# A transformer block's down projection: each of two large buffers holds four residual rows and eight half blocks

## The chip, the cores and the metric

The kernel runs on one core of a Trainium2 chip. A core has five engines that run side by side, each with its own instruction stream: TensorE (PE, matrix products into PSUM banks), VectorE (DVE), ScalarE (ACT), GpSimd (POOL) and SyncE (SP). They wait for each other through semaphores. Sixteen DMA engines move data between HBM and the on-chip memory (SBUF, 128 partitions); here SyncE and GpSimd issue nearly all transfers. The metric is the device time of one launch in microseconds (us), the median of several runs.

## The reference

One layer of a decoder trunk over 1024 tokens of width 1024. A gated mixing sublayer comes first; behind it stands a gated MLP with a short causal convolution, and a residual with layer norm. The change touches the last matrix product and the last two lines:

```python
def conv_ffn(h, w_up, dw_w, dw_b, w_down):
    u = causal_dwconv(h @ w_up, dw_w, dw_b)
    gate, val = jnp.split(u, 2, axis=-1)
    return (jax.nn.silu(gate) * val) @ w_down
...
ffn = conv_ffn(h, w_ffn_up[l], ffn_dw_w[l], ffn_dw_b[l], w_ffn_down[l])
h = layer_norm(DN_ALPHA * h + ffn, ln2_g[l], ln2_b[l])
```

The inner width is 2816 (22 blocks of 128), all data are float32, and `DN_ALPHA` is the fourth root of 2.

## The kernel before

**Products.** A float32 operand is held as two parts, high (a cast, by ScalarE) and low (the rest, by a subtraction on VectorE). `mm3` multiplies high by high, high by low and low by high (L170, L171, L172).

**Up phase.** `up_rest` runs 22 times (j = 0 to 21). Its results `fo` go to scratch in HBM, in a form in which the down phase needs them: `b11_scr`, `b2_scr`, `t32_scr`, `t1_scr`, issued by GpSimd (L995, L997, L1002, L1003).

**Down phase.** `down` computes `@ w_down` by Winograd's form of Strassen's scheme: seven products of half-size operands, p = 0 to 6, in place of eight. Each product has 11 steps k, and a step issues 12 matmuls, three for each of four PSUM banks (128 tokens by 512 columns each). Products 0, 2, 4 and 6 accumulate in the banks X (`acc` 452 to 455), products 1, 3 and 5 in Y (`sm` 456 to 459). After product p the banks are added to the residual rows on VectorE (`own`, L1110; `more`, L1113).

A step's operands come through `load(p, k)`: SyncE fetches a raw tile `dr` (scratch half at L1055, weight half at L1058), GpSimd fetches a second weight block `do` (L1064) for products 0, 1, 4 and 5; VectorE adds them (L1027) into a place that is kept (`c3[k]` in product 0, `c4[k]` in product 1) or in place; ScalarE casts the high part (L1092) and VectorE subtracts for the low part (L1093) of the tile `w_dn`. `dr` has five tiles in turn, so the load of step n + 5 waits until the readers of step n's tile are done. `do` has four, two of them in a pool with the up phase's tiles `s`.

**Big buffers.** A pool `big` holds two buffers of 4 MB each. In the down phase the first holds the eight residual rows (`rows`, read back from `h1_scr` at L1022, eight transfers of 0.5 MB); the second holds the eleven kept blocks `c3`; the `c4` blocks have tiles of their own. Each buffer becomes free when the up phase's tile in it (`h1b1`, `h1b2`) has been read for the last time. The third tile, `last`, takes the next free buffer: it holds the split weights of the last four steps of product 6 (k = 7 to 10).

**The end.** Product 6 runs steps 0 to 2 over all four banks; then, bank by bank, the other eight steps, so that the banks finish one after the other. Product 5's result completes rows 0 to 3, product 6's rows 4 to 7. `ln_out` normalises a row: statistics (L211, L225), square root on ScalarE (L226), reciprocal (L227), two halves each of L231 and L234, and a store of each half to the output by SyncE (L1170).

**Order.** The tile framework schedules the instructions of each engine when the kernel is built, from data dependencies and the priorities in the code; on the chip every engine then keeps its order. DMAs issued by GpSimd go through one queue and those of SyncE through another.

Of the kernel before, what the change touches and what calls it, by code (L numbers as in the profile page):

```python
# [16 lines left out]
P = 128  # L17
# [38 lines left out]
def kernel(  # L56
# [101 lines left out]
    def col_weights(hh, ct):  # L158
        scr = low_scr.get(ct)
        return weights(  # L160
            wcol[ct], f"c{hh}_{ct}", None if hh else scr, scr if hh else None
        )

    def big_tile(name):
# [747 lines left out]
    def up_weights(upp, j):  # L912
# [19 lines left out]
            w3 = split_pair(upp, s3, f"s3_{j}", HALF, 2)  # L932
        return w24, w10, w3

    def up_rest(upp, bl, j, before):

        w24, w10, w3 = up_weights(upp, j)
        ug, uv = (  # L940
            upp.tile([P, T + 32], F32, tag="u", bufs=3, name=f"f{n}{j}") for n in ("ug", "uv")
        )
        s = upp.tile([P, HALF], F32, tag="s", bufs=2, name=f"s{j}")
        SY.dma_start(s, first_scr[j][0])
        SY.dma_start(ug[:, 2 : 2 + HALF], first_scr[j][1])
        G.memset(ug[:, :2], 0.0)
        G.memset(uv[:, :2], 0.0)
        ps, pz = bank(0), bank(0)
        early, late = slice(2, 2 + HALF), slice(2 + HALF, 2 + T)
# [12 lines left out]
        V.tensor_tensor(out=uv[:, early], in0=pz, in1=s, op=ALU.subtract)  # L962
        product(ps, lambda i: w24[:, i, HALF:], bl["b22"], False)
        A.copy(ug[:, late], ps)
        os = []
        j = j // 2 + j % 2 * NK
        for jj, u in ((j, ug), (NF + j, uv)):
            o = upp.tile([P, T], F32, tag="o", bufs=3, name=f"fo{jj}")
            wc = PC_FW + 3 * jj
            A.activation(  # L970
                out=o, in_=u[:, 2 : 2 + T], func=AF.Identity, scale=pc[:, wc + 2 : wc + 3]
            )
            for k in range(2):
                V.scalar_tensor_tensor(
                    out=o,
                    in0=u[:, k : k + T],
                    scalar=pc[:, wc + k : wc + k + 1],
                    in1=o,
                    op0=ALU.mult,
                    op1=ALU.add,  # L980
                )
            os.append(o)
        og, ov = os
        A.activation(out=og, in_=og, func=AF.Silu, bias=pc[:, PC_FB + j : PC_FB + j + 1])
        V.scalar_tensor_tensor(
            out=ov,
            in0=ov,
            scalar=pc[:, PC_FB + NF + j : PC_FB + NF + j + 1],
            in1=og,
            op0=ALU.add,  # L990
            op1=ALU.mult,
        )
        early, late = slice(0, HALF), slice(HALF, T)
        if j < NK:
            G.dma_start(b11_scr[j], ov[:, early])  # L995
            return ov
        G.dma_start(b2_scr[j - NK], ov)  # L997
        a, b, t = before, ov, og
        V.tensor_tensor(out=t[:, early], in0=a[:, late], in1=b[:, late], op=ALU.subtract)
        V.tensor_tensor(out=a[:, late], in0=a[:, early], in1=a[:, late], op=ALU.subtract)  # L1000
        V.tensor_tensor(out=t[:, late], in0=t[:, early], in1=a[:, early], op=ALU.subtract)
        G.dma_start(t32_scr[j - NK], t)  # L1002
        G.dma_start(t1_scr[j - NK], a[:, late])  # L1003

    def down(upp, dp):
# [6 lines left out]
        def flat_big(name):  # L1012
            return big_tile(name).bitcast(F32).rearrange("p i k t -> p (i k t)")

        rows, kept = flat_big("rows"), flat_big("c3")
        c3 = [kept[:, k * HALF : (k + 1) * HALF] for k in range(NK)]
        c4 = [dp.tile([P, HALF], F32, name=f"c4_{k}") for k in range(NK - 1)]
        c4.append(upp.tile([P, HALF], F32, tag="s3", name="c4_last"))
        rs = [rows[:, t * D : (t + 1) * D] for t in range(8)]
        sts = [dp.tile([P, 2, 6], F32, name=f"st_f{t}") for t in range(8)]  # L1020
        for t in range(8):
            G.dma_start(rs[t], h1_scr[t * P : (t + 1) * P, :])  # L1022
        g, b = (row(dp, w, D, n, eng=G) for w, n in ((RW_2G, "ln2_g"), (RW_2B, "ln2_b")))
        E, L = slice(0, HALF), slice(HALF, D)

        def add(dst, x, y):
            V.tensor_tensor(out=dst, in0=x, in1=y, op=ALU.add)  # L1027

        n_steps, n_raw, n_other = 0, 0, 0

        def raw(name):
            nonlocal n_raw
# [1 line left out]
            pl, tag, bufs = ((wst, "st", 3), (upp, "raw", 2))[n_raw % 5 in (1, 3)]  # L1034
            return pl.tile([P, D], F32, tag=tag, bufs=bufs, name=f"{name}_{n_raw}")

        last = []

        def load(p, k):

            nonlocal n_steps, n_other
            a11, a21, a12, a22 = (wdown[h * NK + k, :, cs] for h in range(2) for cs in (E, L))
            x = (
                b11_scr[k],
                b2_scr[k][:, E],
                t32_scr[k][:, L],
                t32_scr[k][:, E],
                t1_scr[k],
                b2_scr[k][:, E],
                b2_scr[k][:, L],  # L1050
            )[p]
            with tc.high_priority(offset=4000):
                st = raw("dr")
                w_st = st[:, E]
                SY.dma_start(st[:, L], x)  # L1055
                w_of = (a11, a12, a22, None, a21, a22, None)[p]
                if w_of is not None:
                    SY.dma_start(w_st, w_of)  # L1058
                o_of = (a21, a22, None, None, a22, t32_scr[k][:, L], None)[p]
                if o_of is not None:  # L1060
                    n_other += 1
                    pl, tag = ((dp, "other"), (upp, "s"))[n_other % 2]
                    other = pl.tile([P, HALF], F32, tag=tag, bufs=2, name=f"do{p}_{k}")
                    G.dma_start(other, o_of)  # L1064
                if p < 2:
                    add((c3, c4)[p][k], w_st, other)
                elif p == 2:
                    add(w_st, w_st, c3[k])
                elif p == 3:
                    w_st = c3[k]  # L1070
                    add(c4[k], c4[k], c3[k])
                elif p == 4:
                    add(w_st, w_st, other)
                elif p == 5:
                    add(st[:, L], st[:, L], other)
                else:
                    w_st = c4[k]
                if p == 6 and k >= NK - 4:
                    if not last:
                        last.append(big_tile("last").rearrange("p i k t -> p (i k t)"))  # L1080
                    w = last[0][:, (k - NK + 4) * 2 * D : (k - NK + 5) * 2 * D]
                    w = w.rearrange("p (i n) -> p i n", i=2)
                else:
                    own = n_steps % 2 and n_steps > 2
                    w = (dp if own else wsp).tile(
                        [P, 2, D], F32R, tag="w", bufs=3, name=f"w_dn{p}_{k}"
                    )
                cuts = ((slice(0, D), st),) if w_st is not c3[k] and w_st is not c4[k] else (
                    (E, w_st), (L, st[:, L])
                )  # L1090
                for cs, src in cuts:
                    A.copy(w[:, 0, cs], src)  # L1092
                    V.tensor_tensor(  # L1093
                        out=w[:, 1, cs], in0=src, in1=w[:, 0, cs].bitcast(F32), op=ALU.subtract
                    )
            n_steps += 1
            return w
# [53 lines left out]
        for p, (banks, first, then) in enumerate(products):  # L1151
            end = NK - LAST if p == 6 else NK
            for k in range(end):
                w = load(p, k)
                for t in range(4):
                    block(banks[t], w, t, first, k)
            ws = {k: load(p, k) for k in range(end, NK)}
            for t in range(4):
                for k in ws:
                    block(banks[t], ws[k], t, first, k)  # L1160
                then(t)
# [143 lines left out]
```

## Time and profile before

| | |
|---|---|
| median of 3 runs | 1967.86 us (1967.69 to 1970.54) |
| the profiled execution | 1962.23 us, of it the span that the trace covers 1960.5 us |
| busy: TensorE, its weight loads, VectorE, ScalarE, GpSimd | 98%, 80%, 82%, 55%, 11% |
| up phase ends, down phase begins | the first matmul of product 0 at 1726.81 us, the last of the up phase at about 1741 |
| last matmul begins, VectorE ends | 1949.74 us, 1957.35 us |

Times in the trace count from the start of the span. The parts of the profile that are used below: busy shares of the engines; a table of stretches of the span with the busy time of each engine, the granted TensorE clock and the load of the DMA engines; a timeline of one engine (start, duration, engine, line, operation, tiles, and in square brackets how long the engine had stood idle and which event ended that); the chain of waits, followed back from the last instruction; and the DMA transfers with their time from issue to landing. An instruction on VectorE or ScalarE shows some 0.1 us more than it keeps the engine, since it overlaps the next: a row's duration may exceed the distance of two starts. The duration 0.39 us of a matmul is its way through the engine; one starts every 0.23 us.

### The profile page before, as it was taken

How to read it: one execution, taken by the hardware profiler on the slowest of the kernel's cores; microseconds unless marked ns; L12 is line 12 of the kernel's file. 1: busy time of each engine (PE TensorE's matmuls, PEld its weight loads, DVE VectorE, ACT ScalarE, POOL GpSimd, SP SyncE). 2: the span in 40 equal slices, each digit the busy share in tenths (PEclk: the TensorE clock that was granted, in tenths of full speed). 3: DMA queues.
4: the chain of work that ended last, by engine and by line, in shares of the span. 5: the costliest groups of instructions: out<-in, count | busy, mean ns of one | idle time of the engine just before them, and what ended most of it. 6: DMA issues, size and time to landing. Idle time of an engine off the chain costs nothing.

```text
span 1960.5 us, 25846 instructions
## 1 busy us (share of the span) xinstructions
PE 1928.3 (98%) x9453; PEld 1572.2 (80%) x9453; DVE 1599.4 (82%) x2224; ACT 1083.5 (55%) x1617; POOL 216.8 (11%) x258
## 2 busy tenths in 40 slices
PE   9999999999999999999999999999999999989997
PEld 7888777777788788888778888888888888868886
DVE  7599999999887548898999646587788888879778
ACT  4666667654263266868775435365555555544432
POOL 0001000111310000110201130001000000121010
PEclk9999999999999999999999999999999999999999
DMA  7645455556446665555554744566445455588673
GB/s 265 223 167 209 162 193 183 172 167 220 142 168 205 211 218 183 191 185 196 190 173 155 233 139 129 176 248 225 167 171 185 165 198 173 184 299 296 196 227 130
DMA packets 127648, 378.36 MB, mean 193 GB/s; under 512 B 15104, under 2 KB 15648, under 8 KB 127520
## 3 DMA queue, kind: packets, MB, share of 16 engines
q1 hardware_dynamic: 107424, 318.48, 48.2%
q0 software_dynamic: 13760, 46.69, 6.9%
q10 hardware_dynamic: 6336, 11.54, 1.6%
q8 instruction: 74, 1.21, 0.2%
q14 instruction: 54, 0.44, 0.1%
HBM read 289.99 MB, written 86.65 MB: 192 GB/s over the span
## 4 chain that ended last, share of the span: by engine, by line
PE 57%; DVE 10%; DMA 5%; ACT 2%; issue 2%; SPq 0%; DVEq 0%; ACTq 0%
PE acc L172 13%; PE acc L171 13%; PE acc L170 13%; PE sm L171 5%; PE sm L172 5%; PE sm L170 5%; DVE c L453 3%; DMA dr<-wdown 1%; DMA dr<-b_scr 1%; DVE w_dn L1093 1%; DMA b_scr<-fo 1%; DVE x L408 1%; PE sm L536 1%; DVE rows L231 1%; DVE rows L234 1%
## 5 line engine op out<-in xcount | busy, mean ns | idle before, releaser
L170 PE MATMUL acc<-hT,w_c 128*128 128x512 f32 x1000 | 391.9, 392 | 0.6 <-ACT x L406 0.6
L172 PE MATMUL acc<-hT,w_c 128*128 128x512 f32 x1000 | 390.2, 391 | 0.6 <-DVE w_c L151 0.5
L171 PE MATMUL acc<-hT,w_c 128*128 128x512 f32 x1000 | 390.6, 391 | 0.0
L453 DVE SCALAR_TENSOR_TENSOR c<-v,pc,c 128x512 f32<-128x512 f32 x480 | 372.2, 801 | 7.1 <-ACT c L442 4.6
L170 PEld LDWEIGHTS acc<-hT,w_c 128*128 128x128 f32 x1000 | 187.8, 188 | 41.6 <-issue 1.9
L172 PEld LDWEIGHTS acc<-hT,w_c 128*128 128x128 f32 x1000 | 187.7, 188 | 41.4 <-DVE w_c L151 1.7
L171 PEld LDWEIGHTS acc<-hT,w_c 128*128 128x128 f32 x1000 | 187.8, 188 | 39.5 <-issue 1.1
L147 ACT CAST w_c<-st_c 128x1024 fp32r<-128x1024 f32 x128 | 133.8, 1045 | 108.9 <-PE acc L172 82.3
L515 POOL TENSOR_TENSOR ce<-ce,xbc 128x1024 f32<-128x1024 f32 x28 | 80.1, 2861 | 678.6 <-ACT ce L514 678.6
L1092 ACT CAST w_dn<-dr 128x1024 fp32r<-128x1024 f32 (+1 forms) x73 | 68.8, 945 | 86.4 <-DMA dr<-wdown 32.8
L504 ACT ACTIVATE m<-ab,acs 128x128 f32<-128x128 f32 x256 | 78.4, 390 | 48.9 <-PE sm L536 47.7
L170 PE MATMUL sm<-h1s,w_s 128*128 128x512 f32 x264 | 102.7, 389 | 0.0
L171 PE MATMUL sm<-h1s,w_s 128*128 128x512 f32 x264 | 102.7, 389 | 0.0
L172 PE MATMUL sm<-h1s,w_s 128*128 128x512 f32 x264 | 102.2, 389 | 0.0
L151 DVE TENSOR_TENSOR w_c<-st_c,w_c 128x1024 fp32r<-128x1024 f32 x64 | 79.0, 1237 | 22.3 <-ACT w_c L147 22.1
L408 DVE SCALAR_TENSOR_TENSOR x<-u,pc,x 128x512 f32<-128x512 f32 x96 | 79.7, 842 | 4.0 <-ACT x L406 3.8
L1093 DVE TENSOR_TENSOR w_dn<-dr,w_dn 128x1024 fp32r<-128x1024 f32 (+1 forms) x73 | 78.6, 1086 | 4.0 <-ACT w_dn L1092 4.0
L172 PE MATMUL acc<-h1b,w_ue 128*128 128x512 f32 x176 | 68.8, 394 | 0.2 <-DVE w_ue L151 0.2
L170 PE MATMUL acc<-h1b,w_ue 128*128 128x512 f32 x176 | 68.6, 390 | 0.0
L171 PE MATMUL acc<-h1b,w_ue 128*128 128x512 f32 x176 | 68.5, 389 | 0.0
L170 PE MATMUL sm<-h1b,w_s 128*128 128x512 f32 x176 | 68.5, 389 | 0.0
L171 PE MATMUL sm<-h1b,w_s 128*128 128x512 f32 x176 | 68.5, 389 | 0.0
(325 smaller groups left out, 4533.9 us busy)
## 6 DMA issues: line engine op xcount, KB each, us to landing
st_c<-wcol SPq DMA_DIRECT2D x128, 512.0 KB, 4.4
low_scr<-w_c SPq DMA_DIRECT2D x64, 512.0 KB, 2.9
w_c<-low_scr SPq DMA_DIRECT2D x64, 512.0 KB, 4.4
ab<-acs_scr SPq DMA_DIRECT2D x32, 512.0 KB, 4.1
dr<-wdown SPq DMA_DIRECT2D x55, 256.0 KB, 5.3
st_wo<-wo SPq DMA_DIRECT2D x24, 512.0 KB, 4.1
st_ue<-wup SPq DMA_DIRECT2D x22, 512.0 KB, 3.9
first_scr<-first ACTq DMA_DIRECT2D x44, 256.0 KB, 3.0
```

Of the source, the lines that this page charges most:

```text
L147: A.copy(w[:, 0, :], st)
L151: V.tensor_tensor(out=w[:, 1, :], in0=st, in1=w[:, 0, :].bitcast(F32), op=ALU.subtract)
L170: TE.matmul(ps, wa(0), xa(0), start=start, stop=False, skip_group_check=more)
L171: TE.matmul(ps, wa(0), xa(1), start=False, stop=False, skip_group_check=more)
L172: TE.matmul(ps, wa(1), xa(0), start=False, stop=stop, skip_group_check=more)
L231: V.scalar_tensor_tensor(out=t, in0=t, scalar=mv[:, i, 0:1], in1=g, op0=ALU.subtract, op1=ALU.mult)
L408: V.scalar_tensor_tensor(out=o, in0=u[:, k : k + HALF], scalar=pc[:, wc + k : wc + k + 1], in1=o, op0=ALU.mult, op1=ALU.add,)
L453: V.scalar_tensor_tensor(out=accs[i], in0=v[:, k : k + HALF], scalar=pc[:, wc + k : wc + k + 1], in1=accs[i], op0=ALU.mult, op1=ALU.add,)
L504: A.activation(out=m[:, h, :], in_=ab[:, h, :], func=AF.Relu, scale=-1.0, bias=acs[:, c, 8 * g + h : 8 * g + h + 1],)
L515: G.tensor_tensor(out=ce, in0=ce, in1=CT[:, cs].unsqueeze(1).to_broadcast([P, 8, P]), op=ALU.mult)
L1092: A.copy(w[:, 0, cs], src)
L1093: V.tensor_tensor(out=w[:, 1, cs], in0=src, in1=w[:, 0, cs].bitcast(F32), op=ALU.subtract)
```

## The change

- Two tiles `rows_c3` and `rows_c4` take the two big buffers. Each holds four residual rows (0 to 3, and 4 to 7) in its first half and eight half blocks in its second: `c3[0]` to `c3[7]` in the first buffer; `c3[8]` to `c3[10]` and `c4[0]`, `c4[1]` in the second. The rest of `c4` keeps tiles of its own.
- Only rows 0 to 3 are loaded at the start. Rows 4 to 7 are loaded in product 2, at its steps 1, 3, 5 and 7, and the two rows of the layer norm (`ln2_g`, `ln2_b`) in product 4. A new function `issue_after` puts each of them behind the newest `do` load in GpSimd's order; it sets the order only, without a semaphore.
- The `do` loads get four buffers of their own in the down phase's pool, and none in the up phase's.
- The last `b11` store (`b11_scr10`) is issued behind the fourth `do` load.
- The weight tile of the fourth step is allocated ahead of all others (`w_dn_own`).

The core of the diff; `issue_after` and the list `stores` are shown at its start, the calls of `load_row` and `load_norm` at its end.

```diff
+    def issue_after(later, earlier):
+
+        tc.add_manual_dep(
+            later.ins,
+            earlier.ins.name,
+            mybir.DependencyInfo(mybir.DependencyClass.NoSync, mybir.DependencyReason.DATA),
+            reason="issue order",
+        )
...
-            G.dma_start(b11_scr[j], ov[:, early])
+            stores.append(G.dma_start(b11_scr[j], ov[:, early]))
...
-        rows, kept = flat_big("rows"), flat_big("c3")
-        c3 = [kept[:, k * HALF : (k + 1) * HALF] for k in range(NK)]
-        c4 = [dp.tile([P, HALF], F32, name=f"c4_{k}") for k in range(NK - 1)]
+        slots = [flat_big(n) for n in ("rows_c3", "rows_c4")]
+        pieces = [[s[:, k * HALF : (k + 1) * HALF] for k in range(8, 16)] for s in slots]
+        c3 = pieces[0] + pieces[1][:3]
+        c4 = pieces[1][3:5]
+        c4 += [dp.tile([P, HALF], F32, name=f"c4_{k}") for k in range(2, NK - 1)]
         c4.append(upp.tile([P, HALF], F32, tag="s3", name="c4_last"))
-        rs = [rows[:, t * D : (t + 1) * D] for t in range(8)]
+        rs = [slots[t // 4][:, t % 4 * D : (t % 4 + 1) * D] for t in range(8)]
         sts = [dp.tile([P, 2, 6], F32, name=f"st_f{t}") for t in range(8)]
-        for t in range(8):
-            G.dma_start(rs[t], h1_scr[t * P : (t + 1) * P, :])
-        g, b = (row(dp, w, D, n, eng=G) for w, n in ((RW_2G, "ln2_g"), (RW_2B, "ln2_b")))
+        g, b = (dp.tile([P, D], F32, name=n) for n in ("ln2_g", "ln2_b"))
+        first_own = dp.tile([P, 2, D], F32R, tag="w", bufs=3, name="w_dn_own")
+
+        def load_row(t):
+            i = G.dma_start(rs[t], h1_scr[t * P : (t + 1) * P, :])
+            if t >= 4:
+                issue_after(i, others[-1])
+
+        for t in range(4):
+            load_row(t)
+
+        def load_norm():
+            for r, start in ((g, RW_2G), (b, RW_2B)):
+                i = G.dma_start(r, prow[start : start + D].partition_broadcast(P))
+                issue_after(i, others[-1])
+
...
-                    n_other += 1
-                    pl, tag = ((dp, "other"), (upp, "s"))[n_other % 2]
-                    other = pl.tile([P, HALF], F32, tag=tag, bufs=2, name=f"do{p}_{k}")
-                    G.dma_start(other, o_of)
+                    other = dp.tile([P, HALF], F32, tag="other", bufs=4, name=f"do{p}_{k}")
+                    others.append(G.dma_start(other, o_of))
+                    if len(others) == 4:
+                        issue_after(stores[-1], others[-1])
...
-                    )
+                    ) if n_steps != 3 else first_own
...
                 w = load(p, k)
+                if p == 2 and k % 2 and k < 8:
+                    load_row(4 + k // 2)
+                elif p == 4 and k == 1:
+                    load_norm()
```

**What it moves.** GpSimd's stream at the end of the up phase, before the change, from the load of the rows on (`fuv`, `fug` and `fo` are tiles of the up phase, `do0_k` is the second block of step k of product 0):

```order
L1022 DMA rows_14232<-h1_scr_115 128x1024 x8
L947 MEMSET fuv20_14026 128x2
L946 MEMSET fug21_14129 128x2
L997 DMA b2_scr9_169<-fo42_13959 128x1024
L1003 DMA t1_scr9_158<-fo31_13819 128x512
L1002 DMA t32_scr9_180<-fo20_13955 128x1024
L1064 DMA do0_0_14268<-wdown 128x512
L947 MEMSET fuv21_14130 128x2
L995 DMA b11_scr10_148<-fo32_14104 128x512
L1064 DMA do0_1_14289<-wdown 128x512
L1064 DMA do0_3_14331<-wdown 128x512
L207 DMA ln2_g_14261<-prow 128x1024
```

And after it:

```order
L1038 DMA rows_c3_14232<-h1_scr_115 128x1024 x4
L958 MEMSET fuv20_14026 128x2
L957 MEMSET fug21_14129 128x2
L1008 DMA b2_scr9_169<-fo42_13959 128x1024
L1014 DMA t1_scr9_158<-fo31_13819 128x512
L1013 DMA t32_scr9_180<-fo20_13955 128x1024
L958 MEMSET fuv21_14130 128x2
L1088 DMA do0_0_14261<-wdown 128x512
L1088 DMA do0_1_14282<-wdown 128x512
L1088 DMA do0_2_14303<-wdown 128x512
L1088 DMA do0_3_14324<-wdown 128x512
L1006 DMA b11_scr10_148<-fo32_14104 128x512
```

The loads of the rows are four and not eight; `do0_0` has gone behind the memset of `fuv21`, `do0_1` to `do0_3` ahead of the store of `b11_scr10`, and the two layer-norm rows are gone from here. Rows 4 to 7 stand behind `do1_10` now, and the layer-norm rows behind `do4_1`.

ScalarE's stream where product 0 begins, before (`w_dn0_0` is the weight tile of the first step, `fo10` and `fo32` are results of the up phase):

```order
L964 COPY fug20_14025<-sm448_14032 128x512
L1092 CAST w_dn0_0_14271<-dr_1_14265 128x1024
L970 ACTIVATE fo10_14100<-fug20_14025,pc_99 128x1024
L970 ACTIVATE fo32_14104<-fuv20_14026,pc_99 128x1024
L1092 CAST w_dn0_1_14292<-dr_2_14286 128x1024
L984 ACTIVATE fo10_14100<-fo10_14100,pc_99 128x1024
```

And after:

```order
L975 COPY fug20_14025<-sm448_14032 128x512
L981 ACTIVATE fo10_14100<-fug20_14025,pc_99 128x1024
L1118 CAST w_dn0_0_14264<-dr_1_14258 128x1024
L981 ACTIVATE fo32_14104<-fuv20_14026,pc_99 128x1024
L995 ACTIVATE fo10_14100<-fo10_14100,pc_99 128x1024
L970 COPY fuv21_14130<-sm450_14136 128x512
L1118 CAST w_dn0_1_14285<-dr_2_14279 128x1024
```

The activation of `fo10` has gone ahead of the cast for the first step, and the cast for the second behind the copy of `fuv21`.

ScalarE's stream behind product 3's last step, before (`w_dn3_10`; `c4_7` to `c4_last` are kept blocks of steps 7 to 10):

```order
L1092 CAST w_dn3_10_15155<-dr_44_15152 128x512
L1092 CAST last_15785<-c4_8_14242 128x512
L1092 CAST last_15785<-c4_last_14244 128x512
L1092 CAST last_15785<-c4_7_14241 128x512
L1092 CAST last_15785<-c4_9_14243 128x512
L1092 CAST w_dn4_0_15182<-dr_45_15176 128x1024
```

And at the end of product 6, before (`rs_f0` to `rs_f3` are the square roots for rows 0 to 3):

```order
L1092 CAST last_15785<-dr_75_15790 128x512
L1092 CAST last_15785<-dr_77_15802 128x512
L1092 CAST w_dn6_5_15771<-c4_5_14239 128x512
L1092 CAST w_dn6_5_15771<-dr_72_15769 128x512
L1092 CAST last_15785<-dr_76_15796 128x512
L1092 CAST w_dn6_6_15778<-c4_6_14240 128x512
L1092 CAST w_dn6_6_15778<-dr_73_15776 128x512
L226 ACT_TABLE_LOAD
L226 ACTIVATE rs_f0_15649<-mv_f0_15648,eps_95 128x1
L226 ACTIVATE rs_f1_15662<-mv_f1_15661,eps_95 128x1
L226 ACTIVATE rs_f2_15675<-mv_f2_15674,eps_95 128x1
L226 ACTIVATE rs_f3_15688<-mv_f3_15687,eps_95 128x1
```

The same engine at the same place, after:

```order
L235 ACTIVATE rs_f0_15647<-mv_f0_15646,eps_95 128x1
L235 ACTIVATE rs_f1_15660<-mv_f1_15659,eps_95 128x1
L235 ACTIVATE rs_f2_15673<-mv_f2_15672,eps_95 128x1
L235 ACTIVATE rs_f3_15686<-mv_f3_15685,eps_95 128x1
L1118 CAST last_15783<-c4_7_14239 128x512
L1118 CAST last_15783<-c4_9_14241 128x512
L1118 CAST last_15783<-c4_8_14240 128x512
L1118 CAST last_15783<-c4_last_14242 128x512
L1118 CAST last_15783<-dr_76_15794 128x512
L1118 CAST last_15783<-dr_75_15788 128x512
L1118 CAST last_15783<-dr_74_15781 128x512
L1118 CAST last_15783<-dr_77_15800 128x512
```

All eight casts into `last` now stand behind the square root for row 3. VectorE's eight subtractions into `last` stand, likewise, behind the last instruction that normalises row 3, and TensorE takes the 84 matmuls of product 6 that read other weight tiles before the 48 that read `last`.

More of the change, by code (lines that the diff above doesn't have):

```diff
@@ L933, in up_weights @@
         return w24, w10, w3
+    stores = []
     def up_rest(upp, bl, j, before):
@@ L1027, in add @@
             V.tensor_tensor(out=dst, in0=x, in1=y, op=ALU.add)
-        n_steps, n_raw, n_other = 0, 0, 0
+        n_steps, n_raw = 0, 0
         def raw(name):
@@ L1035, in raw @@
             return pl.tile([P, D], F32, tag=tag, bufs=bufs, name=f"{name}_{n_raw}")
-        last = []
+        last, others = [], []
         def load(p, k):
-            nonlocal n_steps, n_other
+            nonlocal n_steps
             a11, a21, a12, a22 = (wdown[h * NK + k, :, cs] for h in range(2) for cs in (E, L))
```

## The prediction

> **What bounds the kernel now.** First the page's busy shares, then the table of stretches for the two places where TensorE is not full.
>
> ```profile
> PE 1928.3 (98%) x9453; PEld 1572.2 (80%) x9453; DVE 1599.4 (82%) x2224; ACT 1083.5 (55%) x1617; POOL 216.8 (11%) x258
> ```
>
> ```profile
> 1720.00:1740.00 20.00, 17.28 (x75) 13.68 (x74) 13.75 (x13) 10.98 (x12) 3.36 (x7) 1.00 0.60 230
> 1740.00:1760.00 20.00, 17.32 (x73) 12.99 (x72) 18.37 (x22) 7.58 (x8) 5.47 (x10) 1.00 0.96 329
> 1760.00:1780.00 20.00, 19.49 (x85) 15.57 (x84) 17.00 (x23) 8.41 (x8) 5.20 (x10) 1.00 1.00 357
> 1780.00:1800.00 20.00, 20.00 (x90) 16.56 (x89) 20.00 (x27) 8.43 (x8) 3.55 (x7) 1.00 0.93 323
> ...
> 1920.00:1940.00 20.00, 20.00 (x90) 16.53 (x90) 20.00 (x40) 6.30 (x13) 0.00 (x0) 1.00 0.22 79
> ```
>
> Columns: stretch, length, busy time of PE, its weight loads, DVE, ACT and POOL (instructions in brackets), granted clock, DMA share, GB/s. TensorE is the bound, so time can be won only where it idles: at the start of the down phase (1720 to 1780) and behind the last matmul. From 1920 to 1940 VectorE is full as well. The timeline of PE gives the first matmul of product 0, two of the gaps, and the first of product 2; the pace of a step is read from ScalarE's casts, which TensorE there releases one step at a time.
>
> ```profile
> 1726.81 1.07 PE L170 MATMUL acc<-w_dn 128*128 128x512 f32 x4
> ...
> 1730.82 1.20 PE L170 MATMUL acc<-w_dn 128*128 128x512 f32 x4 [1.14 <-ACT w_dn L1092]
> ...
> 1750.31 1.20 PE L170 MATMUL acc<-w_dn 128*128 128x512 f32 x4 [1.00 <-ACT w_dn L1092]
> ...
> 1800.25 1.07 PE L170 MATMUL acc<-w_dn 128*128 128x512 f32 x4
> ```
>
> ```profile
> 1865.78 1.05 ACT L1092 CAST w_dn<-dr 128x1024 fp32r<-128x1024 f32 x1 [1.67 <-PE acc L172]
> 1868.50 1.05 ACT L1092 CAST w_dn<-dr 128x1024 fp32r<-128x1024 f32 x1 [1.67 <-PE acc L172]
> ```
>
> A step of 12 matmuls takes 2.72 us, one matmul 0.2267. From 1726.81 to 1800.25 TensorE runs products 0 and 1 (22 steps) and the 24 matmuls left of the up phase: 288 x 0.2267 = 65.28 of 73.44 us. **8.16 us are lost there**, and no more than these can be won. The chain of waits says by what:
>
> ```profile
> 1714.68 12.66 DMA b_scr<-fo
> 1727.50 0.47 ACT fo L970
> ...
> 1741.19 0.70 DVE c L1027
> 1741.96 0.32 SPq L1055
> 1742.33 6.82 DMA dr<-wdown
> 1749.21 1.05 ACT w_dn L1092
> ```
>
> ```profile
> 1741.19 1.29 DVE L1027 TENSOR_TENSOR c<-dr,do 128x512 f32<-128x512 f32 x2 [0.41 <-PE sm L172]
> ```
>
> Two waits. A store of the up phase (12.66 us) holds the tile that ScalarE's next activation writes. Then the first sum kept in `c3` waits for a big buffer, whose last reader is a matmul of the up phase. That sum frees the raw tile of `dr_6`, which SyncE therefore loads at 1741.96 only.
>
> **The change at the start.** GpSimd now issues four rows ahead of that store, not eight. Its timeline, the landing time of the rows, and three more stretches:
>
> ```profile
> 1708.23 4.26 POOL L1022 DMA_DIRECT2D rows<-h_scr  x8 [10.28 <-PE acc L172]
> ...
> 1725.54 0.56 POOL L1064 DMA_DIRECT2D do<-wdown  x1 [6.53 <-ACT w_dn L1092]
> ...
> 1737.38 1.09 POOL L1064 DMA_DIRECT2D do<-wdown  x2
> ```
>
> ```profile
> rows<-h_scr POOLq DMA_DIRECT2D x8, 512.0 KB, 10.6
> ```
>
> ```profile
> 1723.00:1728.00 5.00, 5.00 (x24) 4.14 (x23) 2.80 (x3) 1.66 (x3) 0.56 (x1) 1.00 1.03 416
> 1728.00:1733.00 5.00, 2.88 (x12) 1.74 (x10) 4.26 (x4) 3.29 (x4) 0.10 (x1) 1.00 0.42 160
> 1733.00:1738.00 5.00, 4.39 (x19) 3.67 (x20) 4.70 (x6) 3.08 (x4) 1.16 (x3) 1.00 0.01 6
> ```
>
> At 416 GB/s the four rows that go (2 MB) are 5.0 us of a full DMA, so the store lands near 1722.3 in place of 1727.3, and the activation that waited is no longer late. The DMA then lies idle until the loads of product 0 start (share 0.42, then 0.01): the loads had no free tiles and stood behind a store in GpSimd's queue. Now four `do` loads go ahead of the last `b11` store, at about 1728.6 to 1730.8 (GpSimd's memset that waits for the up phase's `fo` at 1732.6 before, less 4 to 5 us, stands ahead of them). They land 5 to 6 us later; the first `c3` sums run near 1736, since `c3[0]` lies in the buffer that has been free since 1708; `dr_6` goes out near 1736.7, 5.3 us earlier. TensorE, unbroken, wants its weights at 1745.9; loaded in 6.82 us and cast and subtracted in 2.2 they stand at 1745.7. Later steps have 1 to 5 us by the same count, and product 2 could begin at 1792.1. At its third step I find a new wait: VectorE must empty product 1's banks first (8.3 us of it behind 1791.0, weights at 1799.3, wanted 1798.4): 0.9 us. **Start: -7.2 us**; the bounds are -8.16 (all of it) and -3 (only the 5 us of the store's wait and what hangs on it, less ScalarE's new order, below).
>
> *Costs that I put at nothing.* Rows 4 to 7 and the two LN rows (3 MB) now ride behind the last `do` of product 1, around 1780 to 1792, beside loads that by the table fill 0.93 of the DMA before; their first reader is product 3, tens of us later, so they can cost only by delaying product 2's weights: 0 to 1 us. Issue slots on GpSimd move and do not grow. The four `other` buffers hold no work back.
>
> **The change at the end.** `last`, the big tile for the weights of the last four steps of product 6, took `c3`'s buffer, free after product 3; half of its casts ran near 1847. Now it takes the buffer of rows 0 to 3, so all 8 casts stand behind the LN of row 3 *and* the landing of the 8 stores of these rows. Rows of VectorE, TensorE, ScalarE and the stores:
>
> ```profile
> 1919.70 0.68 DVE L1113 TENSOR_TENSOR rows<-rows,sm 128x512 f32<-128x512 f32 x1
> ...
> 1938.37 0.67 DVE L1110 SCALAR_TENSOR_TENSOR rows<-rows,acc 128x512 f32<-128x512 f32 x1
> 1938.95 2.73 DVE L234 SCALAR_TENSOR_TENSOR rows<-rows,rs_f,ln_b 128x512 f32<-128x512 f32 x4
> 1941.60 0.69 DVE L211 BATCH_NORM_STATS2 st_f<-rows 128x6 f32<-128x512 f32 x1
> ...
> 1950.32 0.64 DVE L1110 SCALAR_TENSOR_TENSOR rows<-rows,acc 128x512 f32<-128x512 f32 x1
> ...
> 1955.94 1.41 DVE L234 SCALAR_TENSOR_TENSOR rows<-rows,rs_f,ln_b 128x512 f32<-128x512 f32 x2
> ```
>
> ```profile
> 1920.05 0.39 PE L170 MATMUL acc<-w_dn 128*128 128x512 f32 x1
> ```
>
> ```profile
> 1847.05 1.14 ACT L1092 CAST last<-c 128x512 fp32r<-128x512 f32 x2
> 1848.09 1.05 ACT L1092 CAST w_dn<-dr 128x1024 fp32r<-128x1024 f32 x1
> ```
>
> ```profile
> out_dram<-rows SPq DMA_DIRECT2D x16, 256.0 KB, 2.1
> ```
>
> All in before's clock, the start's gain apart. VectorE worked without a pause from 1919.70 to 1941.60, 21.9 us, until row 3 was normalised; 2.4 of them were three `last` subtractions and the first sum of `acc`, which now come later: 19.5. It begins when product 5's first bank is done, 9 matmuls ahead of 1920.05, near 1918.2, so row 3 is ready at 1937.7; its store lands 2.1 to 2.9 later, about **1940.2**. TensorE has 84 matmuls of product 6 that need no `last`: 1920.05 + 19.04 = 1939.1. Its next wants the seventh cast: 7 x 0.52 (two casts take 1.04 from 1847.05 to 1848.09) puts it at 1943.9. **TensorE stands still for 4.8 us.** Its 23rd matmul (5.2 us) completes the first bank at 1949.1. From there VectorE has all of rows 4 to 7 ahead of it: from 1950.32 to the end at 1957.35 it took 7.03, 2.7 of them row 6's, so 4.3 for row 7 with its wait for the square root, 4.0 without; 3 x 4.0 + 4.3 = 16.3. End at 1965.4, not 1957.35: **+8.1 us**; bounds +6 (store 2.0, no other loss) and +10.
>
> *The clock at the restart.* It is a term of its own. The trace has no idle TensorE in mid-kernel that long, but it has both ends:
>
> ```profile
> 1950.00:1955.00 5.00, 0.13 (x1) 0.00 (x0) 4.96 (x11) 0.59 (x2) 0.00 (x0) 0.94 0.39 145
> 1955.00:1960.50 5.50, 0.00 (x0) 0.00 (x0) 2.31 (x5) 0.00 (x0) 0.00 (x0) 0.50 0.42 155
> ```
>
> ```profile
> 3.00:4.00 1.00, 1.00 (x7) 1.00 0.97 389
> ...
> 7.00:8.00 1.00, 1.00 (x12) 1.00 0.99 381
> ```
>
> The last matmul ends at 1950.13 and the clock falls to half: 0.94 over 1950 to 1955 puts the fall near 1954.4, 4.3 us behind it. At the kernel's start (columns: PE, clock, DMA, GB/s) the same transposes run 7 in a us at first and 12 later; the slow part lasts some 4 us. An idle of 4.8 us outlasts 4.3, so I take the restart as cold: 4 us at 7/12 of the pace lose 1.7. Bounds 0 and 2. [...]
>
> **Sum**: -7.2 + 8.1 + 1.7 = **+2.6 us**. Against the profiled execution (1962.23; span 1960.5) that is 1964.8; the runs' median of 1967.86 lies 5.63 above it, for which the trace shows no cause, so I add to the median: **1970.5 us**.
>
> **Rivals.**
> [...]
> 2. *Start not won* (slower). ScalarE's new order puts the up phase's activation ahead of the cast for the very first step. It pays if the store still lands beyond about 1724.8, from where each us is a us of TensorE, up to 2.9; and the loads stay DMA-bound (0.96 to 1.00 in the table). Then the start gives 3 of 7.2: +6.8, 1974.7. Against it: 2 MB fewer on that queue, and 10 us of idle DMA to fill.
> 3. *Faster.* If the 5.63 us that the median lies over the profiled execution are lost in the same starved stretch, the change takes them as well: 2.6 - 5.6 = -3.0, or with a warm restart -4.7: 1964.9 to 1963.2. Nothing in the trace speaks for or against it.
> 4. *The order isn't kept at the end*: some casts into `last` do not wait for the stores (-2.5 us of the stall, and a warm clock): -1.6, 1966.3. Against it: they share one tile.
>
> **Chances.** Forecast 0.42, warm restart 0.20, start not won 0.20, faster 0.10, order not kept 0.08. About 0.2% (3.9 us) is what a measurement of this kernel tells from no change. Slower by more: all but a little of rival 2 and a third of the forecast's spread, 0.33; faster by more: most of rival 3 and a little else, 0.12; the rest, 0.55. The range runs from 1964.8 (rival 3's near end) to 1975.5 (rival 2 with a late store).
>
> **What would show it.** Start: no PE gap between the first matmul of product 0 and product 1; the DMA share of 1733 to 1738 far from 0.01; `dr_6` issued near 1737. End: ScalarE's eight `last` casts in a row near 1933 to 1937 (7.2 us ahead of before's clock), a PE gap of 4 to 5 us before the first matmul on `last`, the first of them 0.4 us apart where they are 0.23 warm, and VectorE ending some 27 us behind the landing of row 3's last store. It is wrong if the gap is under 3 us, or if product 0 still shows gaps of 1 us and more.

## The result, and the profile after

| | before | changed |
|---|---|---|
| median of 22 runs each | 1964.5 us (1960.59 to 1970.54) | 1969.5 us (1965.7 to 1975.55) |
| ratio, 95% interval | 1 | 1.0026 (1.0017 to 1.0034) |
| profiled execution's span | 1960.5 us | 1964.0 us |
| product 0's first matmul to product 6's first (185.1 without a gap) | 193.24 us | 188.11 us |
| product 6's first matmul to VectorE's end | 37.30 us | 47.51 us |

The change makes the kernel 5.1 us slower (0.26% of 1964.5). The last two rows say where: **the start of the down phase gains 5.1 us, its end loses 10.2**; the sum is the measured 5.1. The spans differ by 3.5 only because this execution of the changed kernel reached product 0 1.5 us sooner, at a place that the change doesn't touch.

The start, in the table of stretches of the changed kernel (columns as above):

```profile
1720.00:1740.00 20.00, 19.47 (x87) 15.79 (x86) 18.00 (x19) 13.18 (x14) 4.46 (x9) 1.00 0.51 166
1740.00:1760.00 20.00, 20.00 (x90) 16.57 (x89) 19.91 (x23) 8.94 (x9) 5.60 (x11) 1.00 0.99 345
1760.00:1780.00 20.00, 20.00 (x90) 16.57 (x89) 18.67 (x25) 8.55 (x9) 6.05 (x12) 1.00 0.97 351
1780.00:1800.00 20.00, 18.27 (x81) 14.47 (x79) 18.57 (x26) 5.64 (x6) 3.57 (x7) 1.00 1.03 388
```

PE is full from 1740 to 1780, where it lost time before. New is the gap in the last row, beside a DMA share of 1.03. PE's timeline has all that is left of the start's loss, and product 6's first matmul:

```profile
1725.31 1.07 PE L179 MATMUL acc<-w_dn 128*128 128x512 f32 x4
...
1728.72 0.50 PE L179 MATMUL sm<-h1s,w_s 128*128 128x512 f32 x1 [0.53 <-ACT fuv L970]
...
1797.64 1.21 PE L179 MATMUL acc<-w_dn 128*128 128x512 f32 x4 [0.63 <-ACT w_dn L1118]
1799.95 0.50 PE L180 MATMUL acc<-w_dn 128*128 128x512 f32 x1 [1.09 <-DVE w_dn L1119]
...
1913.42 0.39 PE L179 MATMUL acc<-w_dn 128*128 128x512 f32 x1
```

Counted from start to start the three gaps cost 0.8, 0.8 and 1.5 us (a gap in brackets leaves out the slower start behind it: from the first matmul to the second 0.34 us, at 1728.72 and at 1799.95, where others start 0.23 apart), some 3 us where 8.1 were lost before. At the end the chain of waits goes row by row through the path that the change added:

```profile
1928.54 2.73 DVE rows_c L243 x4
1931.29 2.08 DMA out_dram<-rows_c
1933.62 3.75 ACT last L1118 x7
1937.40 0.50 PE acc L179
```

VectorE normalises rows 2 and 3, the last of their stores lands, ScalarE makes seven casts, and only then TensorE runs on. PE's and VectorE's timelines of the same stretch:

```profile
1937.40 0.50 PE L179 MATMUL acc<-last 128*128 128x512 f32 x1 [4.78 <-ACT last L1118]
1937.74 0.59 PE L180 MATMUL acc<-last 128*128 128x512 f32 x1
1938.13 0.63 PE L179 MATMUL acc<-last 128*128 128x512 f32 x1
1938.56 0.63 PE L180 MATMUL acc<-last 128*128 128x512 f32 x1
...
1941.12 0.44 PE L179 MATMUL acc<-last 128*128 128x512 f32 x1
1941.39 0.39 PE L180 MATMUL acc<-last 128*128 128x512 f32 x1
1941.63 0.40 PE L181 MATMUL acc<-last 128*128 128x512 f32 x1
```

```profile
1944.56 0.69 DVE L1136 SCALAR_TENSOR_TENSOR rows_c<-rows_c,acc 128x512 f32<-128x512 f32 x1 [5.38 <-PE acc L181]
...
1959.51 1.42 DVE L243 SCALAR_TENSOR_TENSOR rows_c<-rows_c,rs_f,ln_b 128x512 f32<-128x512 f32 x2
```

TensorE stands still for 4.78 us. Its next nine matmuls start 0.34 to 0.43 us apart (1937.40 to 1941.12, 3.72 us where nine take 2.04), then 0.27, 0.24 and 0.23. VectorE, which was full from 1920 to 1940 before the change, waits 5.38 us for the first bank and then has 16.4 us of rows 4 to 7 ahead of it.

### The profile page after: what moved, and what is told of

Its sections match the earlier page's. It is cut to its first block, busy times and chain, and to the rows that moved or that the text cites. A ratio compares the mean times of both kernels' runs of the same rounds, so it can differ in the third digit from the quotient of the medians.

```text
span 1964.0 us, 25864 instructions
## 1 busy us (share of the span) xinstructions
PE 1928.4 (98%) x9453; PEld 1574.3 (80%) x9453; DVE 1599.4 (81%) x2224; ACT 1083.3 (55%) x1617; POOL 216.2 (11%) x258
## 4 chain that ended last, share of the span: by engine, by line
PE 60%; DVE 9%; DMA 3%; ACT 3%; issue 1%; DVEq 0%; SPq 0%; ACTq 0%
PE acc L181 13%; PE acc L180 13%; PE acc L179 13%; PE sm L179 6%; PE sm L180 6%; PE sm L181 6%; DVE c L462 3%; DMA dr<-wdown 1%; DVE w_dn L1119 1%; DMA st_wo<-wo 1%; DVE x L417 1%; PE sm L545 1%; DVE rows_c L240 1%; DVE rows_c L243 1%; PE sm L548 0%
```

## The experiments

The table holds for all ten what the sentences below use: the time from product 0's first matmul to product 6's first, less 185.1; the time from there to VectorE's end; and the ratio to the kernel before.

| kernel | lost at the start, us | end, us | ratio (95%) |
|---|---|---|---|
| before | 8.1 | 37.3 | 1 |
| changed | 3.0 | 47.5 | 1.0026 (1.0017 to 1.0034) |
| e1_last_apart | 3.9 | 37.2 | 0.9967 (0.9954 to 0.998) |
| e2_busy_pause | 4.8 | 46.8 | 1.0026 (1.0016 to 1.0036) |
| e3_late_rows_alone | 8.3 | 37.2 | 0.9996 (0.9985 to 1.0007) |
| e4_two_mb_more | 9.4 | 48.0 | 1.0045 (1.0029 to 1.006) |
| e5_apart_and_paced | 0.7 | 38.3 | 0.996 (0.9949 to 0.9971) |
| e6_kept_in_second | 3.4 | 47.5 | 1.0029 (1.002 to 1.0039) |
| e7_rows_as_before | 3.3 | 39.5 | 0.9974 (0.9962 to 0.9986) |
| e7_paced | 1.5 | 39.4 | 0.9961 (0.995 to 0.9973) |
| e8_old_do_tiles | 8.6 | 39.7 | 1.0012 (1.0001 to 1.0024) |
| e9_old_store_order | 5.0 | 39.4 | 0.998 (0.9968 to 0.9992) |

The first two columns are of one execution each, to about 1 us (e1 differs from the changed kernel by 0.9 at a start whose loads and stores stand in the same order). Of the first column 1.7 us in e4, 1.5 in e9 and 0.8 in e7_paced lie in product 5, each around one gap that no edit explains, and some 1.7 in e2 and in e8 are a fall of TensorE's clock in product 2 (last section).

### The end: is it the place of `last`?

e1_last_apart, over the changed kernel; each 4 MB buffer becomes two tiles of 2 MB, here the part of the down phase:

```diff
-        slots = [flat_big(n) for n in ("rows_c3", "rows_c4")]
-        pieces = [[s[:, k * HALF : (k + 1) * HALF] for k in range(8, 16)] for s in slots]
+        slots, kept = [], []
+        for n in ("c3", "c4"):
+            slots.append(flat(f"rows_{n}", 0))
+            kept.append(flat(f"keep_{n}", 1))
+        pieces = [[s[:, k * HALF : (k + 1) * HALF] for k in range(8)] for s in kept]
...
-                    if not last:
-                        last.append(big_tile("last").rearrange("p i k t -> p (i k t)"))
+                    q = k - NK + 4
+                    if q % 2 == 0:
+                        last.append(half_tile(f"last{q // 2}", 1).rearrange("p k t -> p (k t)"))
```

> The changed kernel, but each large buffer is two tiles of 2 MB, rows in one and kept blocks in the other, and `last` takes the two kept-block tiles (free after product 3 and after the second step of product 6). Theory: the whole loss at the end comes from `last` lying where rows 0 to 3 lie. Then TensorE's pause of 4.8 us and its slow restart go, VectorE ends 37.3 us behind product 6's first matmul as before the change (47.5 with it), and only the start's gain of 5.1 us is left: ratio to the kernel before 0.9974 (0.9965 to 0.998), about -5 us. Rival: VectorE's queue at the end is as long in any case because the start's gain only moves the end's work up against it; then it ends more than 42 us behind that matmul and the ratio stays above 1.0.

The whole loss at the end went: 37.2 us, as before the change, and PE has no pause. Its first matmul on `last` and VectorE's last instruction in e1:

```profile
1933.12 0.39 PE L190 MATMUL acc<-last 128*128 128x512 f32 x1
```

```profile
1955.30 1.41 DVE L254 SCALAR_TENSOR_TENSOR rows_c<-rows_c,rs_f,ln_b 128x512 f32<-128x512 f32 x2
```

The rest of the change stands, and the kernel is faster than before it: 0.9967. The rival (VectorE's queue as long in any case) is out.

### The slow restart

e2_busy_pause, over the changed kernel; product 6's matmuls are emitted in two groups, and between them:

```diff
+                spare = bank(0)
+                for _ in range(18):
+                    i = TE.matmul(
+                        spare, ws[6][:, 0, HALF : HALF + P], ws[6][:, 0, :HALF],
+                        start=True, stop=True,
+                    )
+                    issue_after(i, mm)
+                    mm = i
```

> The changed kernel with 18 more matmuls into a free PSUM bank (never read) in TensorE's pause ahead of the first matmul on `last`: 18 x 0.227 = 4.1 us of 4.9. Theory: the restart is slow because TensorE stood still; then the first matmuls on `last` start 0.23 us apart in place of 0.43, the first bank is done 1.8 us earlier and the end comes 1.8 us earlier than in the changed kernel (ratio to the kernel before 1.0016). Rival: the slow start comes from the loads of `last` weights or from something else on TensorE, and the nine slow matmuls stay: no change (1.0026).

PE's timeline in e2, at the same place:

```profile
1941.80 0.50 PE L179 MATMUL acc<-last 128*128 128x512 f32 x1 [0.71 <-ACT last L1118]
1942.13 0.40 PE L180 MATMUL acc<-last 128*128 128x512 f32 x1
1942.37 0.39 PE L179 MATMUL acc<-last 128*128 128x512 f32 x1
```

Kept busy, TensorE restarts at full pace: the first three starts on `last` lie 0.33 and 0.24 us apart, where the changed kernel's first ten lie 0.34 to 0.43 apart. So here the slow matmuls come from its standing still. The time did not follow as expected. Only 0.7 of the 1.8 us show in the end's length (46.8 for 47.5), since the new emission order also changed TensorE's: the first bank is complete with the 28th matmul on `last` and not the 23rd. So the mechanism is shown, and its price in the total isn't: the ratio can't tell 1.0016 from 1.0026 here. In this execution the clock fell at another place too, in product 2 (table of stretches of e2; see the last section):

```profile
1800.00:1803.00 3.00, 1.46 (x5) 0.94 (x6) 2.89 (x5) 1.42 (x2) 0.00 (x0) 0.96 1.02 376
1803.00:1807.00 4.00, 4.00 (x12) 3.17 (x12) 3.36 (x5) 1.99 (x2) 0.00 (x0) 0.60 0.84 282
```

### The start: which part of the change wins there?

e3_late_rows_alone, over the kernel before, takes the late loads alone (`load_row`, `load_norm` and their calls, as in the change's diff). e4_two_mb_more, over the changed kernel, puts their bytes back:

```diff
+        for t in range(4, 8):
+            G.dma_start(slots[0][:, t * D : (t + 1) * D], h1_scr[t * P : (t + 1) * P, :])
```

> The kernel before, with only rows 4 to 7 and the two layer-norm rows loaded late, as the change does; buffers, `do` tiles and the order of stores as before. Theory: the store's wait goes (the two gaps of 1.29 and 1.88 us at product 0's second step), the wait for c3's buffer stays (the gaps near 1750 and 1759, 1.15 and 1.81 us): of the 8.2 us lost at the start 3 are won, ratio 0.9985. Rival: the wait for c3's buffer swallows all of it, since the sixth load is still issued at about 1742: 0 us, ratio 1.0. Second rival: late rows alone give the whole 5.1, ratio 0.9974.

> The changed kernel with four more row loads (2 MB, not used) at the start, into the places that the kept blocks take later, so that as many bytes stand ahead of the up phase's store as before the change. Theory: the store lands some 5 us later again, ScalarE's activation is late, and about 3 us of the start's gain go: ratio to the kernel before 1.004. Rival: the gain at the start is that c3 no longer waits for its buffer, and the bytes ahead of the store don't matter: ratio stays at 1.0026.

In e4 the store takes its 12.5 us again and ScalarE waits for it, as expected, in the chain of waits and on ScalarE's timeline of e4:

```profile
1715.73 12.46 DMA b_scr<-fo
1728.35 0.58 ACT fo L981
```

```profile
1728.35 1.15 ACT L981 ACTIVATE fo<-fug,pc 128x1024 f32<-128x1024 f32 x1 [1.95 <-DMA b_scr<-fo]
```

The start of this execution loses 9.4 us in place of 3.0, more than the 3 us of the theory; the ratio, 1.0045, is near the 1.004 that it gave. Bytes and order came back together, though: the schedule of e4 again puts 24 of product 0's matmuls ahead of the up phase's last 24, as before the change, where the changed kernel has 12 ahead of the first of them and 16 ahead of the last twelve. So e4 shows that the bytes bring the wait back, and not what the bytes alone cost. e3 has the ratio of its first rival (0.9996), but not by its mechanism: the sixth load went out at 1736.7, not at 1742. VectorE's timeline of e3 shows the first `c3` sums:

```profile
1735.90 1.29 DVE L1048 TENSOR_TENSOR c<-dr,do 128x512 f32<-128x512 f32 x2 [0.19 <-PE sm L181]
```

The wait for c3's buffer is over at 1735.9, not 1741.2, with the buffers of before: with the store on time, TensorE itself reaches the up phase's last matmul sooner, 9.7 us behind product 0's first in place of 14.0. By the count of matmuls 1.8 of these 4.3 us are order: 16 of product 0's matmuls stand ahead of it, 24 before. The time is lost later, in products 1 and 2 (PE's timeline of e3):

```profile
1760.12 1.20 PE L179 MATMUL sm<-w_dn 128*128 128x512 f32 x4 [2.06 <-ACT w_dn L1113]
```

```profile
1799.63 0.50 PE L180 MATMUL acc<-w_dn 128*128 128x512 f32 x1 [1.14 <-DVE w_dn L1114]
1803.23 1.21 PE L179 MATMUL acc<-w_dn 128*128 128x512 f32 x4 [1.49 <-ACT w_dn L1113]
```

That overturned a step of mine, so two runs follow. e6_kept_in_second moves c3 back into the late buffer and changes nothing else; every engine's order is that of the changed kernel.

```diff
-        c3 = pieces[0] + pieces[1][:3]
-        c4 = pieces[1][3:5]
+        c3 = pieces[1] + pieces[0][:3]
+        c4 = pieces[0][3:5]
```

> The changed kernel with the kept blocks swapped between the buffers: c3[0] to c3[7] lie in the second buffer, which the up phase frees last, c3[8] to c3[10], c4[0] and c4[1] in the first. Every engine's order is the same. Theory: the first c3 sums wait for the up phase's last matmul again, the sixth raw load goes out near 1741 in place of 1736, and TensorE loses some 3 to 4 us near 1750 and 1759 as before the change; nothing moves at the end: ratio to the kernel before 1.0045. Rival: the loads of the second operand, which go out earlier now, were what mattered, and c3's buffer is free in time either way: ratio stays at 1.0026.

The rival holds. The first sum waits 0.19 us for TensorE and runs at 1736.14, 10.1 us behind product 0's first matmul (1726.04); in the changed kernel it is 9.8 (1735.13 and 1725.31):

```profile
1736.14 0.69 DVE L1053 TENSOR_TENSOR rows_c<-dr,do 128x512 f32<-128x512 f32 x1 [0.19 <-PE sm L181]
```

**The new buffers win nothing at the start.** Then one can do without them. e7_rows_as_before keeps eight rows in one buffer and puts c4[0] and c4[1] behind c3 in the other, to make room for the four `do` tiles:

```diff
-        slots = [flat_big(n) for n in ("rows_c3", "rows_c4")]
-        pieces = [[s[:, k * HALF : (k + 1) * HALF] for k in range(8, 16)] for s in slots]
-        c3 = pieces[0] + pieces[1][:3]
-        c4 = pieces[1][3:5]
+        rows, kept = flat_big("rows"), flat_big("c3")
+        c3 = [kept[:, k * HALF : (k + 1) * HALF] for k in range(NK)]
+        c4 = [kept[:, k * HALF : (k + 1) * HALF] for k in range(NK, NK + 2)]
```

> The changed kernel without its new buffers: the first buffer holds all eight rows again and the second c3[0] to c3[10], with c4[0] and c4[1] behind them (this frees the room that the four `do` tiles need); rows 4 to 7 and the layer-norm rows late, `do` tiles and stores as in the change. Theory after e6: the start's gain owes nothing to the new buffers, and the loss at the end is theirs alone. Then the start loses 3 us of 8.2 as in the changed kernel, TensorE has no pause at `last`, and the ratio to the kernel before is that of e1 (0.9967; 0.9955 to 0.998). Rival: with c3 in the second buffer and `last` in c3's place something of either comes back: ratio above 0.999.

As expected: 0.9974, with 3.3 us lost at the start. The end is 39.5, 2.2 longer than before the change: `last` now waits for c4[1] as well, so four subtractions of 0.6 us that VectorE made behind product 3 come late in product 5. The chain of waits of e7 shows what they hold up:

```profile
1912.55 2.12 DVE last L1118 x4
...
1916.28 2.82 DMA dr<-b_scr
...
1920.39 0.68 DVE rows L1138
```

A raw load goes out behind them, and VectorE waits 2.32 us for the cast of it ahead of its first sum of product 5's result. That sum starts 1.9 us behind product 6's first matmul; before the change it started 0.35 us ahead of it (1919.70 and 1920.05). From this sum to VectorE's end both kernels take 37.65 us. So the full stretch at the end is not longer, it begins later; no run moves the four subtractions alone. e8_old_do_tiles and e9_old_store_order undo one further part of the change in e7:

```diff
-                    other = dp.tile([P, HALF], F32, tag="other", bufs=4, name=f"do{p}_{k}")
+                    pl, tag = ((dp, "other"), (upp, "s"))[(len(others) + 1) % 2]
+                    other = pl.tile([P, HALF], F32, tag=tag, bufs=2, name=f"do{p}_{k}")
```

```diff
-                    if len(others) == 4:
-                        issue_after(stores[-1], others[-1])
```

> e7_rows_as_before with the `do` tiles in two pools of two again, as before the change (the fourth `do` load still ahead of the last b11 store). GpSimd and SyncE then issue some steps' loads out of order (do0_3 ahead of do0_2, step 7 ahead of step 6). Theory: that order is what gave back the gain in e3 (TensorE waits in products 1 and 2), so the ratio rises from e7's to that of e3, about 0.9996. Rival: the order of loads is of no account and the ratio stays at e7's 0.9967.

> e7_rows_as_before without the rule that the last b11 store is issued behind the fourth `do` load. The store then waits on GpSimd for the up phase's last results with do0_1 to do0_3 behind it, 2 to 4 us later than in e7. Theory: their c3 sums come later, so the sixth and seventh raw loads do, and 1 to 2 us of the start's gain go: ratio 0.9975. Rival: those steps have that much room, the ratio stays at e7's 0.9967.

e8 is the answer to e3: with two pools of two tiles the loads of neighbouring steps change places in the schedule, and the start loses 8.6 us again. Some 1.7 of them are a fall of the clock in this execution (granted 0.50 from 1805.16 to 1808.57), but the fall isn't the whole: six of e8's twelve executions have a mean clock of 0.998, as e7's profiled one has, and their median is 1966.3 us where e7's is 1961.6. e8's chain of waits goes through raw loads that landed late:

```profile
1766.18 9.97 DMA dr<-wdown
...
1785.47 12.72 DMA dr<-wdown
```

e9 decides nothing: its interval overlaps e7's, its gaps up to product 2 are e7's, and of the 1.7 us that it loses more in the first column 1.5 lie in product 5 of this execution, around one gap of 1.2.

### The new gap in product 2

e5_apart_and_paced, over e1; e7_paced is the same edit over e7:

```diff
-            i = G.dma_start(rs[t], h1_scr[t * P : (t + 1) * P, :])
+            i = (G if t < 4 else SY).dma_start(rs[t], h1_scr[t * P : (t + 1) * P, :])
             if t >= 4:
-                issue_after(i, others[-1])
+                issue_after(i, raws[-1])
...
-                if p == 2 and k % 2 and k < 8:
+                if p == 3 and k % 2 and k < 8:
```

> e1_last_apart, and rows 4 to 7 come in product 3 and the layer-norm rows in product 4 through SyncE's queue, each behind the raw load of its step, in place of a block of 3 MB behind GpSimd's last `do` load of product 1. In e1 and in the changed kernel TensorE loses 2.3 to 3.2 us in product 2's third to fifth step. Theory: these bytes delay product 2's raw tiles (9.1 us to landing in the changed kernel), so the loss falls under 1 us and the time is 2 us below e1 (ratio to the kernel before 0.9957). Rival: the loss is VectorE's order alone (it empties product 1's banks and takes their statistics ahead of the sums for product 2); then 1.5 us and more of it stay and the ratio is that of e1 (0.9967).

> e7_rows_as_before with rows 4 to 7 and the layer-norm rows paced as in e5. Theory: the same as e5: about 1 us lost at the start, ratio 0.996, the least of all. Rival: a page of its own places c4[0], c4[1] and `last` in one buffer, whose casts come late: above 0.998.

The gap is gone, not only shorter. The table of stretches of e5 at the place where the changed kernel had 18.27:

```profile
1780.00:1800.00 20.00, 20.00 (x90) 16.57 (x89) 20.00 (x28) 6.32 (x7) 2.74 (x5) 1.00 0.86 289
```

and the raw loads of this stretch (1765 to 1802), from issue to landing, in the changed kernel and in e5:

```profile
dr<-wdown SPq DMA_DIRECT2D x13, 256.0 KB, 6.9
```

```profile
dr<-wdown SPq DMA_DIRECT2D x14, 256.0 KB, 5.1
```

The place of the 3 MB is the cause. By which way isn't shown: the raw loads land sooner, but with the late bytes moved the scheduler also put product 2's sums ahead of the emptying of the banks, and the runs don't part the two. The rival, VectorE's order, is not out. **e5 is the fastest, 0.996, and e7_paced equals it (0.9961) with a much smaller edit.** Both beat the kernel before and the changed one.

## Why the prediction was right, and where a step failed

Forecast: +2.6 us, 1970.5, within 0.2% of the kernel before. Measured: +5.1 us (0.26%, just past that line), 1969.5, inside the range. That the two times lie 1.0 us apart is in part luck: the median that the forecast started from was 3.4 us too high and the change 2.5 too small. What happens at the end was right in each step but for the reason given for the clock; the start was over-valued.

- **The end (+8.1 and +1.7 forecast, +10.2 measured).** Its steps held. Row 3 normalised 17.7 us behind product 6's first matmul: 17.8. Its store 2.1 to 2.9: 2.08. TensorE's pause 4.8: 4.78. Slow restart 1.7: 3.72 - 2.04 = 1.7. VectorE's work behind the first bank 16.3: 16.4. e1 shows that all of it hangs on the place of `last`.
- **The clock.** A warm restart, to which the chances gave 0.20, is out: nine matmuls were slow here, and none in e2, where TensorE had work in the pause. In this trace the pause is 4.78 us, the granted clock is 0.50 from 1937.77 to 1941.18, and TensorE was busy for 0.36 of the 3.41 us before the fall.
- **A right result with a wrong reason.** "An idle of 4.8 us outlasts 4.3, so I take the restart as cold": the clock fell 5.1 us behind the last matmul's end (1932.63), 0.4 us after TensorE had started again. The pause did not outlast that time, and the restart was cold all the same. The last section has what the falls went with instead. From its figures I estimate that a pause of 4.78 us is long enough wherever it lies: at worst two stretches of 3.41 us share it and have 2.39 us of it each, which leaves TensorE 1.02 us in each, and with 1.55 (e5) the clock fell. The price varies. In e4 the same pause was followed by ten slow matmuls (1946.36 to 1950.79, 4.43 us where ten take 2.27), 2.2 us lost in place of 1.7.
- **The store's wait: right.** With 2 MB fewer ahead of it the gap at product 0's second step went; e4 brings it back.
- **The start's sum: mis-sized (-7.2 forecast, -5.1 measured).** Two terms. "At its third step I find a new wait: ... 0.9 us" was 2.3, and all of it hangs on the place of the bytes that were to "cost only by delaying product 2's weights: 0 to 1 us": in e5, with these bytes moved, there is no gap, and raw loads take 5.1 us in place of 6.9. And 0.8 us go at a matmul of the up phase that waits for ScalarE's copy of `fuv` (1728.72), a wait that my sum did not have: I had priced ScalarE's new order only for the case of a late store. TensorE's order is new there too, since it takes this matmul one step of product 0 earlier than before, and no run parts the two; e3, with the late loads alone, has the same gap.
- **A reason that was wrong.** "The first `c3` sums run near 1736, since `c3[0]` lies in the buffer that has been free since 1708": the time was right, the "since" was not. e6 has the sums at the same time with c3 in the late buffer. I had taken the two waits of the chain for two causes, but the second was a result of the first: c3's buffer was late because TensorE was, and TensorE was late for the store and for the eight more matmuls of product 0 that stood ahead.
- **A cost that I put at nothing and that was worth the whole gain.** "The four `other` buffers hold no work back": e8 undoes them alone and its ratio, 1.0012, has lost all that e7's 0.9974 had won. By the schedule they keep the loads in step order; that they win by this is argued, not tried apart.
- **The rivals.** *Start not won* did not come by its mechanism, since the store landed in time, though the measured +5.1 lies nearer to its +6.8 than to +2.6. Nor did *faster*: the three runs of before that were at hand had a median of 1967.86, and all 22 have 1964.5, so 3.4 of the 5.63 us over the profiled execution were scatter. *The order isn't kept* did not come either.

## What to carry to other kernels

When tiles are packed into shared buffers, follow not only who can enter sooner but who must wait to leave: the tenant that comes next waits for the slowest one before it, here a layer norm and its stores, and TensorE stood still for 4.78 us. Two waits in one chain are not two causes; ask of the second whether it would still be there if the first were gone, and take one away alone. And ask where bytes land that are moved off a full stretch: here 3 MB came to lie on another full one (DMA share 1.03), and TensorE lost 2.3 us there, which went when e5 and e7_paced loaded them one by one, behind the raw loads of later steps.

## What the runs showed of the hardware that was not expected

TensorE's clock fell without one long pause. In e2 two gaps of 1.0 and 1.4 us (from start to start), 2.3 us apart, were enough: in the stretch from 1800 to 1803 TensorE was busy for 1.46 us of 3.00, and from 1803 to 1807 its granted clock was 0.60 (the rows above). The changed kernel had gaps of 0.8 and 1.5 us at this place and e1 had 1.6 and 1.4, and both kept their clock, so the gaps' length alone doesn't decide it.

The traces show what went with the falls. The changes of the granted clock lie a whole multiple of 3.413 us apart, to 0.01 us: 1937.77, 1941.18 and 1954.84 in the changed kernel (once and four times that length), 1805.16 and 1808.57 in e8 (once), 485.71 and 1946.62 in e5 (428 times). Cut the traces of both kernels and of e1, e2, e5, e6 and e8 into stretches of this length, with a change of the clock at an edge. At full clock, it fell at the end of the stretches in which TensorE was busy for 1.55 us or less, and of none with 1.67 or more: the kernel before, whose emptiest stretch between its first and its last matmul has 1.79, kept its clock until 4.23 us behind the last one. The two nearest cases, from the tables of stretches of e5 (in the up phase) and of e6 (at the pause):

```profile
482.30:485.71 3.41, 1.55 (x7) 1.12 (x7) 3.41 (x5) 3.41 (x5) 0.00 (x0) 1.00 0.23 46
485.71:489.12 3.41, 3.41 (x10) 2.63 (x9) 3.41 (x5) 0.10 (x1) 1.57 (x2) 0.50 0.74 232
```

```profile
1932.09:1935.50 3.41, 1.67 (x8) 1.05 (x6) 0.40 (x2) 0.76 (x2) 0.00 (x0) 1.00 0.58 217
1935.50:1938.92 3.42, 0.39 (x2) 0.34 (x3) 3.42 (x6) 3.42 (x7) 0.00 (x0) 1.00 0.00 0
```

In e2 both gaps lie in one stretch (1799.38 to 1802.79, busy 1.50). In e1 an edge at 1803.67 parts them (busy 2.02 and 2.23), and the changed kernel's stretch with the longer gap has 2.33. In e8 one gap of 2.3 us was enough (1801.75 to 1805.16, busy 1.49). In these traces, then, the falls went with how much of one such stretch was idle, and not with the length of one gap. Each kernel has one trace, so whether the edges lie elsewhere in its other executions isn't shown, nor what happens between 1.55 and 1.67.
